# RG-LRU gates by blocks of 160 channels: permuted channels, stacked remainders, small transfers and another order of outputs

## Chip, core, metric

One Trainium2 chip, one core, one launch. The metric is the device time in microseconds (us). PE is TensorE, DVE VectorE, ACT ScalarE, POOL GpSimd, SP SyncE.

## What is computed

A two-layer network with a context of 256 tokens beside 256 latent tokens: each layer is a feed-forward half step, a mixer and another feed-forward half step, each behind a modulated norm. Layer 0's mixer is the RG-LRU, layer 1's the retention. What concerns the change is the RG-LRU, with 1280 channels in 8 gate blocks of 160:

```python
def block_diag(x, w, b):
    xg = x.reshape(bsz, t, LRU_BLOCKS, LRU_BLK)          # 8 blocks of 160
    return (jnp.einsum('btgi,gij->btgj', xg, w) + b).reshape(bsz, t, D_RNN)

def lru_coeffs(xc, gate_w, gate_b, lam):
    r = jax.nn.sigmoid(block_diag(xf, gate_w[0], gate_b[0]))
    ig = jax.nn.sigmoid(block_diag(xf, gate_w[1], gate_b[1]))
    log_a = -LRU_C * r * jax.nn.softplus(-lam)
    a = jnp.exp(log_a)
    b = jnp.sqrt(-jnp.expm1(2.0 * log_a)) * (ig * xf)
...
    # xc = conv of 4 taps over time of h @ w_x; for each of two directions d
    # h_t = a_t * h_(t-1) + b_t, the latent scan starting from the context's end
    # y = ((hs_forward + hs_backward) * gelu(h @ w_g)) @ w_out
```

## The kernel before, in words

Activations are transposed: 128 channels on the partitions, 512 columns (256 of context, 256 latent). The 1280 channels of the RG-LRU are 10 columns j of 128. Each product with a weight block is three fp32r products on PE (`mm3`, lines 142 to 144): weight high by activation high, high by low, low by high. Weights come from HBM as tiles of 8 blocks, 128x1024 (`w_fetch`, SP's queue); `w_ahead` keeps LA = 2 tiles split ahead: ACT copies the high part (`whi`, line 112), DVE subtracts for the low part (`wlo`, line 138, `w_low`). There are four buffers each of raw, high and low.

The RG-LRU stage (`lru`) runs per column: two input projections (`wx`, `wg`, 8 blocks each), a convolution of four taps (`conv`: ACT copies the sums out of PSUM into a padded buffer, line 587, and makes the first tap, line 588; DVE adds three more, line 583; ACT and DVE split the result, lines 592 and 595), the gates, ACT's functions and DVE's vector steps. Since 160 is not 128, a column of gates meets two or three columns of inputs (`gate_rows`): 26 pairs of columns, times 4 gates (r and i for two directions), times 3 products = 312. ACT's functions of a column are gelu, sigmoid (line 627), exp (632), tanh (635) and square root (642), with four loads of tables. DVE's vector steps are lines 655 to 663 with two scans (648; 650 and 651 backwards), then Y is split into high (ACT, 668) and low (DVE, 671). Of r there are three buffers, of i one, of a and s two.

The order is written by hand. Steps of ACT wait in the list `bga`, steps of DVE in `bgv`; each time PE takes up a weight block, `pump` issues one step of each list if the step's `ready` allows. So a queue's order is fixed at build time, and each engine takes its instructions in that order. The output product (`out_proj`, which adds to the residual on DVE, line 401, two halves of 256 columns) runs for columns [0, 1] before the gates of column 6, for [2 to 5] behind all gates, and for [6 to 9] as the `boundary` to the next feed-forward, by halves of 256 columns, with four weight tiles held for the second half and the statistics of the next norm (`stat`, line 311) behind it.

Of the kernel before, what the change touches and what calls it, by code (L numbers as in the profile page):

```python
# [71 lines left out]
NTILES = 371  # L72


class Kernel:
    def __init__(self, tc, aps):
        self.tc, self.nc, self.aps = tc, tc.nc, aps
# [15 lines left out]
        self.rate = 1  # L93
        self.bga, self.bgv = deque(), deque()
# [9 lines left out]
    def w_ahead(self, t):  # L104
        nc = self.nc
        self.w_fetch(min(t + LA + DA + 1, NTILES))
        while self.nsplit < min(t + LA + 1, NTILES):
# [6 lines left out]
            self.wlow.append((lo, raw, hi))  # L114
# [20 lines left out]
    def w_low(self):  # L135
        while self.wlow:
            lo, raw, hi = self.wlow.popleft()
            self.nc.vector.tensor_tensor(lo, raw, hi.bitcast(F32), ALU.subtract)  # L138
# [226 lines left out]
    def out_proj(self, acts, key, layer, gidx, halves, st=None, hooks=None, tick=0, hold=False):  # L365
# [6 lines left out]
        for hi_, (c0, c1) in enumerate(halves):  # L372
            w = c1 - c0
            def part(ps, d, lo, hi):
                for i in range(lo, hi):
                    if hi_ and hold:
                        whi, wlo = held[(i, d)]
                    else:
                        whi, wlo = held[(i, d)] = self.w(key(i, d))
                    ah, al = acts[i](c0, c1)  # L380
                    self.mm3(ps[:, :w], whi, wlo, ah, al, i == 0, i == na - 1)
            early = {}
            if hi_ == 0 and na > 1:
# [3 lines left out]
            for d in range(KD):  # L387
# [3 lines left out]
                else:  # L391
                    ps = self.psum()
                    part(ps, d, 0, na)
                if st is not None and d:
# [17 lines left out]
    def boundary(self, acts, key, layer, gidx, nl, nn, x_only=False, hold=False):  # L412
# [30 lines left out]
        self.out_proj(acts, key, layer, gidx, [(0, T), (T, 2 * T)], st=st, hold=hold, hooks={  # L443
# [98 lines left out]
    def lru(self, hooks):  # L542
        nc, tc = self.nc, self.tc
        xc, xs, gl, Y = {}, {}, {}, {}
# [15 lines left out]
        banks = self.first_group([wx(0), wx(1), wg(0), wg(1)], False, hooks)  # L560
# [6 lines left out]
        gb = self.vec("gb").rearrange("p (j g) -> p j g", j=NR)  # L567
        sp4, sp8 = self.sp4, self.sp8
        cbuf = [pool.tile([P, 2, T + 3], F32, name="cbuf%d" % i) for i in range(2)]
        for c in cbuf:  # L570
            nc.vector.memset(c[:, :, 0:1], 0.0)
            nc.vector.memset(c[:, :, T + 1:T + 3], 0.0)

        def conv(j, ps):
            buf = cbuf[j % 2]
            p3 = ps.rearrange("p (s t) -> p s t", s=2)
            x = pool.tile([P, 512], F32, tag="xc", name="xc", bufs=3)
            x3 = x.rearrange("p (s t) -> p s t", s=2)
            s = pool.tile([P, 2, 512], F32R, tag="xs", name="xs", bufs=3)
            xc[j], xs[j] = x, s  # L580

            def tap(w):
                nc.vector.scalar_tensor_tensor(x3, buf[:, :, w:w + T], cw[:, j, w:w + 1], x3,  # L583
                                               op0=ALU.mult, op1=ALU.add)

            def first():
                nc.scalar.activation(buf[:, :, 1:T + 1], p3, AF.Copy)
                nc.scalar.activation(x, ps, AF.Identity, bias=cb[:, j:j + 1], scale=cw[:, j, 1:2])
                tap(0)

            def high():
                nc.scalar.activation(s[:, 0], x, AF.Copy)

            def low():
                nc.vector.tensor_tensor(s[:, 1], x, s[:, 0].bitcast(F32), ALU.subtract)
                convdone.add(j)
            return [first, lambda: tap(2), lambda: tap(3), high, low]

        def gelu(j, ps):
            g = self.tmp("gl")  # L600
            nc.scalar.activation(g, ps, AF.Gelu_apprx_tanh)
            gl[j] = g

        def gates(j):
            rows = gate_rows(j)
            out = [self.psum() for _ in range(4)]
            for n, i in enumerate(rows):
                for dg in range(4):
                    whi, wlo = self.w(("lg", dg // 2, dg % 2, i, j))
                    if i not in convdone:  # L610
                        self.bg_until(lambda: i in convdone)
# [3 lines left out]
        def coeffs(j, ps, pgs):  # L615

            b = {}
            stt, tt = nc.vector.scalar_tensor_tensor, nc.vector.tensor_tensor
            act = nc.scalar.activation

            def new(tag, bufs):
                b[tag] = pool.tile([P, 2, 512], F32, tag=tag, name=tag, bufs=bufs)
                return b[tag]

            def sig(d, g):
                t = b[("r", "i")[g]] if d else new(*(("r", 3), ("i", 1))[g])
# [558 lines left out]
```

## Time and profile before

| | |
|---|---|
| time, median of 3 runs | 1883.34 us (1883.06 to 1883.91) |
| the profiled execution | 1883.77 us |
| its span | 1882.0 us |
| granted PE clock, mean | 0.993 |
| PE, DVE, ACT busy | 1854.5 (99%), 1283.0 (68%), 718.0 us (38%) |
| chain that ended last | PE 92%, DVE 5%, ACT 1%, issue 1% |

A busy PE is one whose products follow on one another; their ends are modelled, so their pace is read from the starts. The shares over the whole span are averages of stages with different limits: the RG-LRU stage lies from 423.6 to about 652 us of the span, and its own rows are below. A wait is the idle time of an engine ahead of an instruction, with the last instruction that released it.

### The profile page before, as it was taken

How to read it: one execution, taken by the hardware profiler on the slowest of the kernel's cores; microseconds unless marked ns; L12 is line 12 of the kernel's file. 1: busy time of each engine (PE TensorE's matmuls, PEld its weight loads, DVE VectorE, ACT ScalarE, POOL GpSimd, SP SyncE). 2: the span in 40 equal slices, each digit the busy share in tenths (PEclk: the TensorE clock that was granted, in tenths of full speed). 3: DMA queues.
4: the chain of work that ended last, by engine and by line, in shares of the span. 5: the costliest groups of instructions: out<-in, count | busy, mean ns of one | idle time of the engine just before them, and what ended most of it. 6: DMA issues, size and time to landing. Idle time of an engine off the chain costs nothing.

```text
span 1882.0 us, 25737 instructions
## 1 busy us (share of the span) xinstructions
PE 1854.5 (99%) x10282; PEld 1620.9 (86%) x10284; DVE 1283.0 (68%) x2108; ACT 718.0 (38%) x984; POOL 0.2 (0%) x4
## 2 busy tenths in 40 slices
PE   8999999999999899999999999999999999999998
PEld 7888888897888788888889888888898899999998
DVE  7877697676899975767577655455576465575555
ACT  3322222248989342222224322222243243344443
POOL 0000000000000000000000000000000000000000
PEclk8999999999999999999999999999999999999999
DMA  8355454422322244454442445454324433355553
GB/s 320 130 213 183 168 189 181 145 90 79 101 90 90 79 157 168 157 178 177 149 161 98 151 160 176 151 179 165 106 71 158 135 113 112 101 168 176 183 191 101
DMA packets 77736, 277.52 MB, mean 147 GB/s; under 512 B 8752, under 2 KB 10032, under 8 KB 77616
## 3 DMA queue, kind: packets, MB, share of 16 engines
q1 hardware_dynamic: 77616, 275.88, 42.6%
q8 instruction: 80, 1.31, 0.3%
q14 instruction: 40, 0.33, 0.1%
HBM read 274.80 MB, written 1.05 MB: 147 GB/s over the span
## 4 chain that ended last, share of the span: by engine, by line
PE 92%; DVE 5%; ACT 1%; issue 1%; DMA 0%; SPq 0%; ACTq 0%; DVEq 0%
PE ps L142 30%; PE ps L144 30%; PE ps L143 30%; PE ps L237 1%; DVE x L401 1%; DVE wlo L138 1%; DVE acc L290 1%; DVE hlo L138 1%; DVE h L360 0%; ACT h L354 0%; PE ps L335 0%; DVE ht L352 0%; PE ps L302 0%; DMA x<-xt 0%; DVE xc L583 0%
## 5 line engine op out<-in xcount | busy, mean ns | idle before, releaser
L142 PE MATMUL ps<-h,whi 128*128 128x512 f32 (+1 forms) x1824 | 640.8, 351 | 0.0
L143 PE MATMUL ps<-h,whi 128*128 128x512 f32 (+1 forms) x1824 | 640.2, 351 | 0.6 <-DVE h L360 0.5
L144 PE MATMUL ps<-h,wlo 128*128 128x512 f32 (+1 forms) x1824 | 639.5, 351 | 1.2 <-DVE wlo L138 1.2
L138 DVE TENSOR_TENSOR wlo<-wraw,whi 128x1024 fp32r<-128x1024 f32 x349 | 417.7, 1220 | 78.4 <-ACT whi L112 78.2
L112 ACT ACTIVATE whi<-wraw 128x1024 fp32r<-128x1024 f32 x349 | 357.2, 1049 | 275.4 <-PE ps L143 225.7
L144 PEld LDWEIGHTS ps<-h,wlo 128*128 128x128 f32 x1824 | 345.7, 190 | 47.7 <-DVE wlo L138 1.9
L143 PEld LDWEIGHTS ps<-h,whi 128*128 128x128 f32 x1824 | 345.7, 190 | 46.3 <-DVE h L360 1.7
L142 PEld LDWEIGHTS ps<-h,whi 128*128 128x128 f32 x1824 | 345.7, 190 | 45.2 <-ACT h L354 0.3
L242 DVE SCALAR_TENSOR_TENSOR junk<-modraw,cB 128x1024 bf16<-128x1024 f32 x240 | 293.1, 1221 | 4.6
L401 DVE SCALAR_TENSOR_TENSOR x<-ps,M,x 128x256 f32<-128x256 f32 x296 | 132.5, 479 | 159.4 <-PE ps L144 158.9
L157 ACT ACTIVATE A<-sil 128x512 fp32r<-128x512 f32 (+1 forms) x88 | 50.9, 579 | 474.3 <-DVE sil L494 474.3
L142 PE MATMUL ps<-A,whi 128*128 128x512 f32 (+1 forms) x608 | 217.9, 358 | 0.0
L143 PE MATMUL ps<-A,whi 128*128 128x512 f32 (+1 forms) x608 | 217.9, 358 | 0.0
L144 PE MATMUL ps<-A,wlo 128*128 128x512 f32 (+1 forms) x608 | 217.9, 358 | 0.0
L494 DVE TENSOR_TENSOR sil<-ps,sil 128x512 f32<-128x512 f32 (+1 forms) x88 | 54.8, 622 | 159.9 <-PE ps L144 152.0
L144 PEld LDWEIGHTS ps<-A,wlo 128*128 128x128 f32 x608 | 114.9, 189 | 17.0
L142 PEld LDWEIGHTS ps<-A,whi 128*128 128x128 f32 x608 | 114.9, 189 | 16.7
L143 PEld LDWEIGHTS ps<-A,whi 128*128 128x128 f32 x608 | 114.9, 189 | 16.7
L158 DVE TENSOR_TENSOR A<-sil,A 128x512 fp32r<-128x512 f32 (+1 forms) x88 | 55.1, 626 | 56.7 <-ACT A L157 56.7
L493 ACT ACTIVATE sil<-ps 128x512 f32<-128x512 f32 (+1 forms) x88 | 47.2, 537 | 80.4 <-PE ps L144 79.9
L354 ACT ACTIVATE h<-ht,M 128x256 fp32r<-128x256 f32 x88 | 42.4, 504 | 89.5 <-DVE ht L352 89.5
L142 PE MATMUL ps<-A,hhi 128*128 128x256 f32 x192 | 54.8, 285 | 0.0
(173 smaller groups left out, 2061.1 us busy)
## 6 DMA issues: line engine op xcount, KB each, us to landing
wraw<-w SPq DMA_DIRECT2D x371, 512.0 KB, 4.3
modraw<-modw SPq DMA_DIRECT2D x144, 512.0 KB, 4.3
x<-xt SPq DMA_DIRECT2D x8, 256.0 KB, 5.1
mask<-mask SPq DMA_DIRECT2D x4, 512.0 KB, 5.9
out<-fin SPq DMA_DIRECT2D x8, 128.0 KB, 1.8
cs<-rope SPq DMA_DIRECT2D x1, 256.0 KB, 2.6
vecs<-vecs SPq DMA_DIRECT2D x1, 251.0 KB, 6.5
ident<-ident SPq DMA_DIRECT2D x1, 64.0 KB, 2.0
```

What stands on the lines that cost most here:

```text
L112: nc.scalar.activation(hi, raw, AF.Copy)
L138: self.nc.vector.tensor_tensor(lo, raw, hi.bitcast(F32), ALU.subtract)
L142: mm(ps, whi, xhi, start=first, stop=False, skip_group_check=True)
L143: mm(ps, whi, xlo, start=False, stop=False, skip_group_check=True)
L144: mm(ps, wlo, xhi, start=False, stop=last, skip_group_check=True)
L157: self.nc.scalar.activation(hi, src, AF.Copy)
L158: self.nc.vector.tensor_tensor(lo, src, hi.bitcast(F32), ALU.subtract)
L242: nc.vector.scalar_tensor_tensor(self.junk, raw, 1.0, self.cB[:, c, :], op0=ALU.mult, op1=ALU.mult, accum_out=M[:, idx, k, c:c + 1])
L354: nc.scalar.activation(h[:, 0, a:b], tt, AF.Identity, bias=M[:, 3 * n, k, c:c + 1])
L401: nc.vector.scalar_tensor_tensor(self.x[d][:, a0:a1], ps[:, a0 - c0:a1 - c0], M[:, gidx, d, c:c + 1], self.x[d][:, a0:a1], op0=ALU.mult, o ...
L493: nc.scalar.activation(s[:, :w], pa[:, c0:c1], AF.Silu)
L494: nc.vector.tensor_tensor(s[:, :w], pg[:, c0:c1], s[:, :w], ALU.mult)
```

## The change

The channels of the RG-LRU are permuted: columns 0 to 7 are the first 128 channels of blocks 0 to 7, columns 8 and 9 the remaining 32 of blocks 0 to 3 and 4 to 7. The gates of a block are then five outputs: four of 128 (the gates) and one that holds the 32 remaining outputs of all four gates. Each gets one `mm3` from the block's own column and a single product with 96 rows from `S`, in which the 32 remainder channels stand three times (high, low, high) against weights stacked as high, high, low (kind "ls"; `w_low` makes their low part in rows 64 to 96 of the high tile, so that a weight tile with both kinds is split in two or three pieces on DVE). S is filled by three transfers of 64 KB per block and the fifth output's gates go to the remainder columns' r and i by four, all issued on POOL (56 in all). A gate is a tanh of half the argument, with the factors moved into the steps behind it; the taps of the convolution read PSUM directly; r has two buffers; three tiles are split ahead in the stage. The outputs run for [0, 1], for [2, 3, 8], for [4, 5, 6] as sums that stay in eight PSUM banks (`out_sum`), and the boundary adds [7, 9] to these, with two tiles held.

```diff
+LRU_PERM = np.concatenate([np.arange(160 * b, 160 * b + P) for b in range(8)]
+                          + [np.arange(160 * b + P, 160 * b + 160) for b in range(8)])
+LRU_ORDER = (0, 1, 2, 3, 8, 4, 5, 6, 7, 9)
...
+    def out_sum(self, acts, key):
+        banks = [self.psum() for _ in range(KD)]
+        for i, act in enumerate(acts):
+            for d in range(KD):
+                self.mm3(banks[d], *self.w(key(i, d)), *act(0, 2 * T), i == 0, False)
+        return banks
...
-        banks = self.first_group([wx(0), wx(1), wg(0), wg(1)], False, hooks)
+        banks = self.first_group([wx(8), wx(0), wx(1), wg(0)], False, hooks)
+        self.la = LA + 1
...
             def first():
-                nc.scalar.activation(buf[:, :, 1:T + 1], p3, AF.Copy)
-                nc.scalar.activation(x, ps, AF.Identity, bias=cb[:, j:j + 1], scale=cw[:, j, 1:2])
+                act(x, ps, AF.Identity, bias=cb[:, j:j + 1], scale=cw[:, j, 1:2])
                 tap(0)
...
+        def stack_x(b):
+            t = S[b] = pool.tile([P, 512], F32R, tag="S", name="S", bufs=2)
+            src = xs[8 + b // 4]
+            q = slice(32 * (b % 4), 32 * (b % 4) + 32)
+            for i, part in enumerate((0, 1, 0)):
+                nc.gpsimd.dma_start(t[32 * i:32 * i + 32], src[q, part])
...
-        def gates(j):
-            rows = gate_rows(j)
-            out = [self.psum() for _ in range(4)]
-            for n, i in enumerate(rows):
-                for dg in range(4):
-                    whi, wlo = self.w(("lg", dg // 2, dg % 2, i, j))
...
-                    self.mm3(out[dg], whi, wlo, xs[i][:, 0], xs[i][:, 1], n == 0, n == len(rows) - 1)
+        def gates(b):
+            out = [self.psum() for _ in range(5)]
+            for g in range(5):
+                self.mm3(out[g], *self.w(("lg", b, g)), xs[b][:, 0], xs[b][:, 1], True, False)
+            for g in range(5):
+                w, _ = self.w(("ls", b, g))
+                nc.tensor.matmul(out[g], w[0:96], S[b][0:96], start=False, stop=True, skip_group_check=True)
+            if b % 4 < 2:
+                stack_x(b + 2)
...
+        def gate_rem(b, ps):
+            t = self.tmp("rem")
+            act(t, ps[4], AF.Tanh, bias=self.gbr[:, b:b + 1], scale=0.5)
+            q = slice(32 * (b % 4), 32 * (b % 4) + 32)
+            for g in (0, 2, 1, 3):
+                nc.gpsimd.dma_start((R, I)[g % 2][8 + b // 4][q, g // 2], t[32 * g:32 * g + 32])
...
+            out += [with_ready(lambda: (alloc(b, R, "r", 2), gate(b, 0, ps)),
+                               lambda c: c < 2 or c - 2 in ydone, b), lambda: gate(b, 2, ps)]
...
-        out([2, 3, 4, 5])
-        js = [6, 7, 8, 9]
+        out([2, 3, 8])
...
+        js = [4, 5, 6]
+        self.bg_until(lambda: all(j in ydone for j in js))
+        banks = self.out_sum(acts(js), okey(js))
+        js = [7, 9]
...
-        self.hold |= {first + 2, first + 3, first + 6, first + 7}
-        return self.boundary(acts(js), okey(js), 0, 5, 0, 2, hold=True)
+        self.hold |= {first + 4, first + 5}
+        return self.boundary(acts(js), okey(js), 0, 5, 0, 2, hold=True, banks=banks)
```

Three places show how the rows of an engine move (line numbers of before and of the change differ). ACT's queue at the start of the stage; before, with lines 587 to 592 as the convolution:

```order
L587 ACTIVATE cbuf_3401<-ps 128x2x256
L588 ACTIVATE xc<-ps,vecs 128x512
L592 ACTIVATE xs<-xc 128x512
L587 ACTIVATE cbuf_3402<-ps 128x2x256
L588 ACTIVATE xc<-ps,vecs 128x512
L592 ACTIVATE xs<-xc 128x512
L601 ACT_TABLE_LOAD
L601 ACTIVATE gl<-ps 128x512 x2
L112 ACTIVATE whi<-wraw 128x1024 x3
```

and now, with lines 614 and 619 as the convolution, 639 as gelu:

```order
L614 ACTIVATE xc<-ps,vecs 128x512
L619 ACTIVATE xs<-xc 128x512
L614 ACTIVATE xc<-ps,vecs 128x512
L619 ACTIVATE xs<-xc 128x512
L614 ACTIVATE xc<-ps,vecs 128x512
L619 ACTIVATE xs<-xc 128x512
L639 ACT_TABLE_LOAD
L639 ACTIVATE gl<-ps 128x512
L114 ACTIVATE whi<-wraw 128x1024 x4
```

Three convolutions stand ahead of the first gelu instead of two, each without its copy, and four weight splits instead of three follow. ACT's queue at one column's functions before (627 gates, 632 exp, 635 tanh, 642 square root):

```order
L627 ACTIVATE r<-ps,vecs 128x512 x2
L627 ACTIVATE i<-ps,vecs 128x512 x2
L112 ACTIVATE whi<-wraw 128x1024
L587 ACTIVATE cbuf_3401<-ps 128x2x256
L588 ACTIVATE xc<-ps,vecs 128x512
L632 ACT_TABLE_LOAD
L632 ACTIVATE a<-r,sp_647 128x512 x2
L635 ACTIVATE r<-r,sp_646 128x512 x2
L592 ACTIVATE xs<-xc 128x512
L642 ACT_TABLE_LOAD
L642 ACTIVATE s<-r 128x1024
L112 ACTIVATE whi<-wraw 128x1024 x2
```

and now at block 3, which brings columns 3 and 8 (656 gates, 661 the fifth output, 682 exp, 685 tanh, 689 square root):

```order
L656 ACTIVATE i<-ps,gbh 128x512
L661 ACTIVATE rem<-ps,gbr 128x512
L682 ACT_TABLE_LOAD
L682 ACTIVATE a<-r,sp_647 128x512 x2
L619 ACTIVATE xs<-xc 128x512
L682 ACTIVATE a<-r,sp_647 128x512 x2
L685 ACTIVATE r<-r,sp_646 128x512 x4
L689 ACT_TABLE_LOAD
L689 ACTIVATE s<-r 128x1024
L114 ACTIVATE whi<-wraw 128x1024
L689 ACTIVATE s<-r 128x1024
L114 ACTIVATE whi<-wraw 128x1024
```

Exp, tanh and square root of two columns follow one another, and the weight splits stand behind a square root. DVE's queue there before (650 to 663 end column 2's steps, 138 is the weights' low part, 655 the first step of the next column):

```order
L650 SCALAR_TENSOR_TENSOR r<-a,s 128x256
L651 SCALAR_TENSOR_TENSOR r<-a,r,s 128x256
L662 TENSOR_TENSOR r<-r 128x512
L595 TENSOR_TENSOR xs<-xc,xs 128x512
L663 TENSOR_TENSOR r<-r,gl 128x512
L138 TENSOR_TENSOR wlo<-wraw,whi 128x1024 x2
L655 TENSOR_TENSOR i<-i,xc 128x1024
```

and now (719 to 732 end column 2's steps, 153 and 151 are the pieces of the weights' low parts, 724 is the first step of column 3):

```order
L719 SCALAR_TENSOR_TENSOR r<-a,s 128x256
L720 SCALAR_TENSOR_TENSOR r<-a,r,s 128x256
L731 TENSOR_TENSOR r<-r 128x512
L732 TENSOR_TENSOR r<-r,gl 128x512
L622 TENSOR_TENSOR xs<-xc,xs 128x512
L153 TENSOR_TENSOR wlo<-wraw,whi 128x896
L151 TENSOR_TENSOR whi<-wraw,whi 32x128
L724 SCALAR_TENSOR_TENSOR r<-a,r 128x1024
```

In place of two whole tiles, the two pieces of one split tile stand ahead of the next column's first step; the rest follows behind it.

## Rows read from the trace of the kernel before

**Rows 1.** The table of busy times by stretch, in us. Columns: stretch, its length, busy time of PE, PEld, DVE, ACT and POOL with the number of instructions in brackets, granted PE clock, DMA share, GB/s.

```profile
454.00:500.00 46.00, 46.00 (x203) 37.81 (x202) 40.36 (x45) 40.05 (x50) 0.00 (x0) 1.00 0.31 103
500.00:560.00 60.00, 60.00 (x264) 49.38 (x264) 55.75 (x72) 53.73 (x67) 0.00 (x0) 1.00 0.30 97
560.00:612.00 52.00, 52.00 (x229) 42.78 (x229) 48.70 (x59) 49.12 (x61) 0.00 (x0) 1.00 0.26 81
```

**Rows 2.** The waits from 454 to 628 us, from the first column's vector steps to the last Y: waiting engine, tile and line, what it waited for; us in total, times, longest us.

```profile
ACT Y L668 <- DVE r L663: 12.3, 1, 12.3
...
DVE wlo L138 <- ACT whi L112: 5.1, 5, 1.5
...
DVE xs L595 <- ACT xs L592: 3.4, 3, 1.6
DVE xc L583 <- ACT xc L588: 3.0, 4, 1.0
```

**Rows 3.** DVE's timeline in the first column's vector steps: start us, busy us, engine, line, operation (x2 or x3: so many in a row).

```profile
454.04 1.22 DVE L655 TENSOR_TENSOR i<-i,xc 128x1024 f32<-128x1024 f32 x1
...
462.66 1.22 DVE L138 TENSOR_TENSOR wlo<-wraw,whi 128x1024 fp32r<-128x1024 f32 x1
463.80 2.32 DVE L583 SCALAR_TENSOR_TENSOR xc<-cbuf,vecs,xc 128x512 f32<-128x512 f32 x3
466.04 0.69 DVE L663 TENSOR_TENSOR r<-r,gl 128x512 f32<-128x512 f32 x1
```

**Rows 4.** DVE's timeline around the last Y low and the first statistic of the boundary, columns as in rows 3; behind a start in square brackets the idle time before it and who ended it.

```profile
626.03 0.87 DVE L401 SCALAR_TENSOR_TENSOR x<-ps,M,x 128x256 f32<-128x256 f32 x2
626.82 0.68 DVE L671 TENSOR_TENSOR Y<-r,Y 128x512 fp32r<-128x512 f32 x1
627.42 0.87 DVE L401 SCALAR_TENSOR_TENSOR x<-ps,M,x 128x256 f32<-128x256 f32 x2
...
642.37 0.16 DVE L311 TENSOR_SCALAR rs_m<-ps 128x2 f32<-128x2 f32 x1 [0.30 <-PE ps L302]
```

**Rows 5.** PE's timeline at the start of the stage (512-column products) and at the end of the next ffn's first group (256-column products, then the next 512-column ones), columns as in rows 3. The ends of products are modelled and overlap; the starts tell the pace.

```profile
423.61 0.40 PE L142 MATMUL ps<-h,whi 128*128 128x512 f32 x1
...
424.30 0.40 PE L142 MATMUL ps<-h,whi 128*128 128x512 f32 x1
...
428.85 0.39 PE L144 MATMUL ps<-h,wlo 128*128 128x512 f32 x1
...
677.42 0.28 PE L144 MATMUL ps<-h,hlo 128*128 128x256 f32 x1
677.54 0.40 PE L142 MATMUL ps<-h,whi 128*128 128x512 f32 x1
```

**Rows 6.** ACT's timeline, columns as in rows 3: the first convolution of the stage and the start of the second, and one column's scalar steps later on (a: exp, r: tanh, s: square root).

```profile
423.87 0.60 ACT L587 ACTIVATE cbuf<-ps 128x512 f32<-128x512 f32 x1 [5.63 <-PE ps L144]
424.36 0.77 ACT L588 ACTIVATE xc<-ps,vecs 128x512 f32<-128x512 f32 x1
...
428.12 0.58 ACT L587 ACTIVATE cbuf<-ps 128x512 f32<-128x512 f32 x1
...
560.24 0.72 ACT L632 ACTIVATE a<-r,sp 128x512 f32<-128x512 f32 x1
560.85 1.33 ACT L635 ACTIVATE r<-r,sp 128x512 f32<-128x512 f32 x2
562.20 1.28 ACT L642 ACT_TABLE_LOAD   x1
563.49 1.06 ACT L642 ACTIVATE s<-r 128x1024 f32<-128x1024 f32 x1
564.46 0.61 ACT L592 ACTIVATE xs<-xc 128x512 fp32r<-128x512 f32 x1
564.98 1.99 ACT L112 ACTIVATE whi<-wraw 128x1024 fp32r<-128x1024 f32 x2
...
571.86 1.27 ACT L627 ACTIVATE r<-ps,vecs 128x512 f32<-128x512 f32 x2
573.01 1.26 ACT L627 ACTIVATE i<-ps,vecs 128x512 f32<-128x512 f32 x2
```

**Rows 7.** The groups of instructions by line and form; number of instructions, busy us, mean ns of one, idle before. The gate products of line 142 (lines 143 and 144 have as many).

```profile
L142 PE MATMUL ps<-xs,whi 128*128 128x512 f32 x104 | 41.1, 395 | 0.5 <-ACT xs L592 0.5
```

**Rows 8.** The same view, columns as in rows 7, of three kinds of DVE operation.

```profile
L401 DVE SCALAR_TENSOR_TENSOR x<-ps,M,x 128x256 f32<-128x256 f32 x296 | 132.5, 479 | 159.4 <-PE ps L144 158.9
...
L360 DVE SCALAR_TENSOR_TENSOR h<-ht,M,h 128x256 fp32r<-128x256 f32 x88 | 41.7, 481 | 8.1 <-ACT h L354 8.1
...
L658 DVE TENSOR_SCALAR a<-r 128x1024 f32<-128x1024 f32 x10 | 6.9, 687 | 0.0
```

**Rows 9.** The page's table of transfers: what, queue, number, KB each, median us from issue to landing.

```profile
out<-fin SPq DMA_DIRECT2D x8, 128.0 KB, 1.8
...
vecs<-vecs SPq DMA_DIRECT2D x1, 251.0 KB, 6.5
ident<-ident SPq DMA_DIRECT2D x1, 64.0 KB, 2.0
```

**Rows 10.** The table of busy times by stretch again, columns as in rows 1, of two stretches of 4 us at the end of the stage.

```profile
620.00:624.00 4.00, 0.67 (x3) 0.67 (x4) 3.93 (x7) 0.00 (x0) 0.00 (x0) 0.65 0.01 2
624.00:628.00 4.00, 3.86 (x18) 3.55 (x18) 3.93 (x8) 1.85 (x3) 0.00 (x0) 0.50 0.41 131
```

More of the change, by code (lines that the diff above doesn't have):

```diff
@@ L566, in lru @@
         cb = self.vec("cb")
[L567 to L572, printed above, removed]
-        def conv(j, ps):
[L575 to L580, printed above, removed]
+        gb = self.gbh.rearrange("p (j g) -> p j g", j=NR)
@@ L654, in coeffs @@
             sv = [
[L655 to L659 removed]
+                lambda: stt(r, a, 1.0, r, op0=ALU.add, op1=ALU.mult),
@@ L673, in coeffs @@
[L673 to L695 removed]
+                tt(Y[c][:, 1], r[:, 0], Y[c][:, 0].bitcast(F32), ALU.subtract)
@@ L696, in vector_steps @@
+                ydone.add(c)
+            sv[1:1], sv[5:5] = tail[:1], tail[1:]
             tail = [high, low]
             self.bgv.extend(sv)
-        for j in range(NR):
-            pgs = []
-            if j == 6:
-                out([0, 1])
-            n = j + 2 if j < 6 else j + 1
-            if j != 6 and n < NR:
-                pgs.append((n, self.proj(wg(n), 0, 2 * T)))
-            g = gates(j)
-            self.drain()
-            if prev is not None:
-                vector_steps(prev)
-            prev = coeffs(j, g, pgs)
-            self.bga.extend([lambda: None] * (3 if j else 0) + prev[0])
-            if j + 2 < NR:
-                px = self.proj(wx(j + 2), 0, 2 * T)
-                c = conv(j + 2, px)
-                rest = list(self.bgv)
-                self.bgv.clear()
-                self.bgv.extend(c[:3] + rest[:1] + c[3:4] + rest[1:2] + c[4:] + rest[2:])
@@ L718, in lru, with out @@
-        prev[1][0].ready = lambda: not self.bga
-        vector_steps(prev)
-        self.bgv.extend(tail)
-        out([2, 3, 4, 5])
-        js = [6, 7, 8, 9]
+        def out(js):
+            self.bg_until(lambda: all(j in ydone for j in js))
+            self.out_proj(acts(js), okey(js), 0, 5, [(0, 2 * T)])
+        for n, j in enumerate((8, 0, 1)):
+            self.bgv.extend(conv(j, banks[n]))
+        while self.bgv:
+            self.pump()
+        gelu(0, banks[3])
+        pgs = [(1, self.proj(wg(1), 0, 2 * T))]
@@ new lines, in lru @@
+        todo = ((("x", 2), ("g", 2)), (("x", 3), ("x", 9)), (("x", 4), ("g", 3)), (("x", 5), ("g", 8)),
+                (("x", 6), ("g", 4)), (("x", 7), ("g", 5)), (("g", 6), ("g", 7), ("g", 9)), ())
+        prev = []
+        for b in range(8):
+            if b == 6:
+                out([0, 1])
+            self.bg_until(lambda: b in convdone and 8 + b // 4 in convdone)
+            g = gates(b)
+            self.bg_until(lambda: not self.bga)
+            for c in prev:
+                vector_steps(c)
+            self.bga.extend(scalar_steps(b, g, pgs))
+            prev = [b] + ([8 + b // 4] if b % 4 == 3 else [])
+            pgs = []
+            for kind, n in todo[b]:
+                if kind == "x":
+                    c = conv(n, self.proj(wx(n), 0, 2 * T))
+                    rest = list(self.bgv)
+                    self.bgv.clear()
+                    self.bgv.extend(c[:4] + rest[:3] + c[4:] + rest[3:])
+                else:
+                    pgs.append((n, self.proj(wg(n), 0, 2 * T)))
@@ L723, in lru @@
+        out([2, 3, 8])
+        self.bg_until(lambda: not self.bga)
+        for c in prev:
+            vector_steps(c)
+        self.bgv.extend(tail)
+        self.la = LA
+        js = [4, 5, 6]
+        self.bg_until(lambda: all(j in ydone for j in js))
+        banks = self.out_sum(acts(js), okey(js))
+        js = [7, 9]
         self.drain()
```

245 lines of the change are left out of this document (139 added, 106 removed).

## Prediction

> **What bounds it now.** Three views, in this order. The table of busy times by stretch [rows 1] covers the RG-LRU stage: PE is busy in every microsecond from 454 to 612, so PE sets the pace there. The same rows put DVE at 40.36 of 46.00, 55.75 of 60.00 and 48.70 of 52.00 us: the second queue is about 90% full, and what is taken from PE can be gained only until DVE is full. The waits between the first column's vector steps and the last Y [rows 2] then say how full DVE is: in 173.4 us, from the first step at 454.04 [rows 3] to the end of the last Y low at 627.42 [rows 4], DVE waited 5.1 + 3.4 + 3.0 = 11.5 us on ACT and about 1.0 on others; 173.4 - 11.5 - 1.0 = 160.9 us is its own work. Last, the timelines [rows 3 to 6] give the length of each step. I measure from T0 = 423.61, where the stage's first 512-column product starts [rows 5]: first vector step T0 + 30.4, last Y low T0 + 203.8, first product after the next ffn's first group (677.54) T0 + 253.9.
>
> **PE.** The gates lose 312 - 160 = 152 products (104 for each of three lines before [rows 7]; now 8 blocks of 20). In a run of them the starts are 4.55 us apart for 20 intervals, from 424.30 to 428.85 [rows 5]: 0.2275 each, 152 x 0.2275 = 34.6 us; the output phases change by -0.5. If PE were still the bound the stage would end 35.1 us sooner. It can't be: DVE has some 158 us in a stretch that would be left with 138. So PE gets idle time, over 40 us of it, and while that lasts what PE does differently costs nothing. The 40 single products with 96 rows are not in this trace; I take them as 0.2275 [rows 5]. Ends: 0.12, the start spacing at the 256-column products (677.42 to 677.54 [rows 5]), and twice that 0.2275, 0.46; that is -4.3 to +9.1 us of PE time, which the idle time covers.
>
> **DVE's own work, first step to last Y low.** The nine vector steps of a column have the same sizes, the same ten times. Two more pairs of output additions fall in it (16 for 14): 0.79 a pair (626.03 to 626.82 [rows 4]), +1.6. Of the weights' low parts there are 19 whole tiles and 15 pieces of 7 more, where there were 28 tiles: 1.14 a tile (462.66 to 463.80 [rows 3]), a piece by its width plus some 0.07 to start (twice the 0.60 of 512 columns, 626.82 to 627.42 [rows 4], is 0.06 over 1.14), -1.7. One convolution fewer: three taps 2.24 (463.80 to 466.04 [rows 3]) and a low part of 0.6, -2.9. The taps now read PSUM: the addition that reads PSUM takes 479 ns, its like in SBUF 481 [rows 8], so no cost; ends 0 and, with 0.1 for each tap, +1.8. Sum: 160.9 + 1.6 - 1.7 - 2.9 = 158, rounded.
>
> **Start.** ACT and DVE take three convolutions in turn before any gate instead of two. One took 4.25 (423.87 to 428.12 [rows 6]), of which the copy into the buffer, 0.49, goes: 3.8 each, so ACT is free at T0 + 11.8 instead of T0 + 8.9. Behind it stand the table load 1.3, two gelus 1.0, five weight splits 4.75, r and i 2.3, the remainder 0.6, a load 1.3, exp 1.25, a convolution's first step 0.65, tanh 1.25, a load 1.3, square root 1.0, xs 0.6 (rows alike in [rows 6]): T0 + 29.1; two more splits 1.9, 0.35 to hand over, and three pieces on DVE, 1.3: the first vector step at T0 + 32.7, 2.3 later.
>
> **ACT's waits, the term that decides.** R has two buffers instead of three. ACT may start block b's gates only after the Y low of column b - 2, and that stands inside column b - 1's steps on DVE. ACT's queue has r, i, remainder, exp, tanh, square root and only then the weight split whose low part stands on DVE *ahead* of the next column's steps. So DVE runs out of work while ACT goes through the chain.
> - Block 3 brings two columns. ACT from the Y low: r 1.15, i 1.2, a split 0.95, first conv step 0.65, remainder 0.6, load 1.3, exp 1.24, xs 0.5, waiting for the transfers 1.0, exp of column 8 1.24, four tanh 2.5, load 1.3, square root 0.97, split 0.95: 15.6. DVE has 10.2 to do meanwhile (9.2 of work, 1.0 counted with the short waits): it waits 5.4.
> - Block 6: r 1.15, i 1.15, remainder 0.6, split 0.95, load 1.3, exp 1.24, tanh 1.24, load 1.3, root 0.97, split 0.95 = 10.85, against 7.4: 3.4.
> - Block 7, two columns again: 15.8 against 10.1: 5.7.
> - First column 2.9, and eight short waits for convolution and splits, 6.3 in all.
>
> Sum 23.7, where 11.5 was. For the transfers I take 2.0 us each, the 64 KB row in [rows 9], two behind one another; ends 1.8 and 6.5, the fastest and the slowest kind of large transfer [rows 9]. Table loads fall from 42 to 27 in the program, 15 x 1.28 = 19 us of ACT; they lie beside DVE's work except for two in each of the three chains, where I counted them.
> Last Y low: 32.7 + 158 + 23.7 + 1.0 = T0 + 215.4, **11.6 later** than T0 + 203.8.
>
> **The end of the stage.** Y low to the first statistic took 14.95 (627.42 to 642.37 [rows 4]). Now [4,5,6] are summed in eight PSUM banks beforehand and only [7,9] follow, so no third phase of additions stands behind the last Y on DVE, and two held tiles are split there instead of four: 11.4, and 32.2 instead of 34.3 for the rest, up to the next ffn's second group. Together -5.6. The engine clock is in this: PE was busy 0.67 of 4 us from 620 on and was then granted 0.50 of full speed, the lower of its two levels, from 624 to 628 [rows 10]; I assume the same for the new gap before [7,9].
>
> **Sum:** +11.6 - 5.6 = +6.0. The profiled execution took 1883.77, 0.43 over the median of 1883.34; on the median that gives 1889.3, on the profiled one 1889.8; I say **1889.5**.
>
> **The skill against the trace.** Each chain above holds two table loads at 1.28 us. In the row the load begins at 562.20, just as the tanh pair ends (560.85 + 1.33), and the root follows at 563.49 [rows 6]. The Trainium skill (ScalarE: Activation LUTs, section What ACT_TABLE_LOAD costs) has a drain of some 1.38 us beside the load's 1.28; by that each long wait would be 2.8 longer and the sum some +14. The trace shows the load but no such pause around it, so the row stands.
> Transfers issued from POOL are new; the trace of before has none. The Trainium skill (SBUF — State Buffer, box The "DVE blocks DMA" trap) says that their descriptors are written by GpSimd, which is locked out while DVE runs an operation in its fast two-port mode, and advises another queue; it speaks against this change. In this trace only the subtraction from a constant, 687 ns [rows 8] against 1.22 us for the others of that size [rows 3], looks like such a mode, once per column. That becomes a rival below.
>
> **Rivals.** All hang on w, the sum of DVE's waits on ACT: the time is 1889.5 + (w - 23.7). A measurement of this kernel tells 0.2%, 3.8 us, from no change.
> 1. *The chain as above*, w over 21.5: slower. For it: two R buffers and the split behind the root are fixed by the order. Chance 0.45; 1887 to 1897.
> 2. *Late transfers*: at 6.5 instead of 2.0 each, two in turn put 9 us more before the exponentials of column 8 and again of column 9, and DVE has nothing else: 1889.5 + 18 = 1907. It decides when a transfer of 64 KB takes over about 3. Chance 0.09.
> 3. *A smaller excess*: the slots of ACT and DVE overlap better, w from 13.9 to 21.5; within 0.2%. Chance 0.20.
> 4. *The other side: the waits stay at 11.5*, because pieces and convolutions on DVE fill the chains and ACT, with 19 us of loads and ten copies of 0.49 less, gets ahead by the time of block 3. Then Y low is at T0 + 203.2, -0.6, and with -5.6 the sum is -6.2: 1877. It decides if w is under 13.9. For it: ACT waited 12.3 in one piece for DVE already before, near the end [rows 2], so it is not always the late one; against it: the two buffers, which tie ACT to the Y low whatever else it saves. Chance 0.21.
> 5. *DVE never waits*: w = 0, -17.7, 1866; beyond it no gain is possible while DVE's 158 stand. Anything from 1873 down: 0.05.
>
> Faster 0.21 + 0.05 = 0.26, same 0.20, slower 0.45 + 0.09 = 0.54. The range 1873 to 1900 leaves out case 5 and most of case 2, and the far end of case 1. The forecast's own range is 1887 to 1897: each chain may be off by 1.5 us, the taps add up to 1.8, and a longer gap at half clock on PE some 2 more.
>
> **What would show it.** Right: PE's busy share from T0 to T0 + 215 near 77%; DVE's waits on ACT some 24 us, in three long pieces of 3 to 6 us on the weights' low part, at blocks 3, 6 and 7; ACT's r gates waiting for Y low; last Y low near 639 on the trace's clock; the next ffn's second group near 683.5; POOL's transfers near 2 us. Wrong: PE as busy as before (a product costs more than 0.2275), waits under 14 us, or POOL's transfers over 3 us with ACT's exp waiting for them. A change before 423 or behind 690 would be one that I have not seen.

## The result and the profile after

The changed kernel took 1901.82 us (median of 4, 1899.63 to 1902.13) against 1883.24: ratio 1.0096, 95% interval 1.0078 to 1.0113, **18.6 us slower**. The forecast was slower, 1889.5, 6 us over before; the measured time lies outside the range of 1873 to 1900 and the change is three times the one forecast.

The profiled execution (1902.07 us, span 1900.3) shows the loss in the RG-LRU stage. PE's first 512-column product of the stage and the one behind the next feed-forward's first group (start, length, engine, line, operation), which answer to [rows 5]:

```profile
424.12 0.40 PE L158 MATMUL ps<-h,whi 128*128 128x512 f32 x1
...
695.69 0.40 PE L158 MATMUL ps<-h,whi 128*128 128x512 f32 x1
```

271.57 us lie between them, where 253.93 did. DVE's timeline in the first column's steps, at its longest waits (idle time and releaser in square brackets), at the last Y low and the first statistic answers to [rows 3, 4]:

```profile
458.65 1.22 DVE L724 SCALAR_TENSOR_TENSOR r<-a,r 128x1024 f32<-128x1024 f32 x1
459.90 0.69 DVE L725 TENSOR_SCALAR a<-r 128x1024 f32<-128x1024 f32 x1
460.51 1.22 DVE L726 SCALAR_TENSOR_TENSOR i<-i,xc 128x1024 f32<-128x1024 f32 x1
461.76 1.23 DVE L727 TENSOR_TENSOR s<-s,i 128x1024 f32<-128x1024 f32 x1
...
521.44 1.09 DVE L153 TENSOR_TENSOR wlo<-wraw,whi 128x896 fp32r<-128x896 f32 x1 [5.68 <-ACT whi L114]
...
595.62 1.23 DVE L153 TENSOR_TENSOR wlo<-wraw,whi 128x1024 fp32r<-128x1024 f32 x1 [3.80 <-ACT whi L114]
...
608.90 0.88 DVE L428 SCALAR_TENSOR_TENSOR x<-ps,M,x 128x256 f32<-128x256 f32 x2 [5.36 <-PE ps L160]
609.70 0.68 DVE L740 TENSOR_TENSOR Y<-r,Y 128x512 fp32r<-128x512 f32 x1
...
625.73 1.23 DVE L153 TENSOR_TENSOR wlo<-wraw,whi 128x1024 fp32r<-128x1024 f32 x1 [5.23 <-ACT whi L114]
...
650.38 0.69 DVE L740 TENSOR_TENSOR Y<-r,Y 128x512 fp32r<-128x512 f32 x1 [0.69 <-ACT Y L737]
...
662.39 0.16 DVE L327 TENSOR_SCALAR rs_m<-ps 128x2 f32<-128x2 f32 x1 [0.37 <-PE ps L318]
```

From the stage's start at 424.12 the first vector step comes at +34.5 (predicted 32.7), the end of the last Y low, 650.38 + 0.61 = 650.99, at +226.9 (predicted 215.4; before 203.8). The three long waits for the weights' high part are there with almost the forecast sizes, 5.68, 3.80 and 5.23 (forecast 5.4, 3.4, 5.7). What was not forecast stands between them: 5.36 us in which DVE waits for PE at an addition of the outputs (608.90), with column 5's Y low (609.70) queued behind it. The waits between the first step and the last Y low (in all, times, longest), which answer to [rows 2]:

```profile
ACT r L656 <- DVE Y L740: 21.3, 5, 6.6
DVE wlo L153 <- ACT whi L114: 18.2, 9, 5.7
...
DVE x L428 <- PE ps L160: 5.4, 1, 5.4
...
DVE xc L611 <- ACT xc L614: 3.7, 3, 2.0
...
DVE xs L622 <- ACT xs L619: 2.3, 3, 1.4
...
DVE Y L740 <- ACT Y L737: 0.7, 1, 0.7
```

DVE's waits on ACT sum to 18.2 + 3.7 + 2.3 + 0.7 = 24.9 us (forecast 23.7, before 11.5). PE's row says why it no longer sets the pace, and in what state it is (stretch, PE, PEld, DVE, ACT, POOL busy, clock, DMA share, GB/s):

```profile
458.65:650.99 192.34, 155.66 (x614) 121.64 (x612) 159.56 (x201) 124.57 (x157) 19.66 (x40) 0.90 0.30 90
```

PE is busy 155.66 of 192.34 us at a mean granted clock of 0.90, against 1.00 in [rows 1].

### The profile page after: what moved, and what is told of

Read it like the earlier page. It is cut to its first block, busy times and chain, and to the rows that moved or that the text cites. A ratio compares the mean times of both kernels' runs of the same rounds, so it can differ in the third digit from the quotient of the medians.

```text
span 1900.3 us, 25479 instructions
## 1 busy us (share of the span) xinstructions
PE 1837.1 (97%) x10084; PEld 1598.2 (84%) x10084; DVE 1283.7 (68%) x2117; ACT 694.2 (37%) x956; POOL 27.8 (1%) x60
## 4 chain that ended last, share of the span: by engine, by line
PE 63%; DVE 6%; ACT 3%; issue 2%; DMA 0%; POOL 0%; ACTq 0%; DVEq 0%
PE ps L159 21%; PE ps L160 21%; PE ps L158 21%; DVE wlo L153 1%; ACT whi L114 1%; ACT r L685 0%; DVE i L726 0%; DVE s L727 0%; ACT h L370 0%; DVE h L376 0%; DVE r L724 0%; DVE x L428 0%; DVE hlo L153 0%; ACT a L682 0%; DVE acc L306 0%
## 5 line engine op out<-in xcount | busy, mean ns | idle before, releaser
L153 DVE TENSOR_TENSOR wlo<-wraw,whi 128x1024 fp32r<-128x1024 f32 (+2 forms) x350 | 411.7, 1199 | 88.9 <-ACT whi L114 88.4
L158 PE MATMUL ps<-Y,whi 128*128 128x512 f32 (+1 forms) x96 | 39.8, 415 | 21.0 <-DVE x L428 8.9
```

Of the source, the lines that this page charges most:

```text
L153: sub(lo[:, c], raw[:, c], hi[:, c].bitcast(F32), ALU.subtract)
L158: mm(ps, whi, xhi, start=first, stop=False, skip_group_check=True)
```

## The experiments

Each time is a median; before took 1883.2 to 1883.6 beside them. The 95% intervals of the ratios reach about 2.8 us to each side (some 1.8 with ten runs), so a difference of 1 or 2 us between two medians is not read as an effect. Theory A going in: r's two buffers tie ACT's gates to the Y low, and DVE's waits follow. Rivals: PE with its gaps and lower clock (B), ACT's own order (C).

**r freed early.**

```diff
-                               lambda c: c < 2 or c - 2 in ydone, b), lambda: gate(b, 2, ps)]
+                               lambda c: c < 2 or c - 2 in rdone, b), lambda: gate(b, 2, ps)]
...
-                lambda: tt(r[:, 0], r[:, 0], gl[c], ALU.mult),
+                lambda: (tt(gl[c], r[:, 0], gl[c], ALU.mult), rdone.add(c)),
```

> Edit: the column's last product writes into gelu's tile instead of r, Y is split from there, and r counts as free at that product, some 5 us of DVE work before the Y low. Theory A (r's two buffers tie ACT's gates to the Y low; DVE's waits, PE's gaps and the half clock follow from that): the three long waits of DVE for the weights' high part (5.7, 3.8, 5.2 us) fall under 1.5 each, DVE's waits on ACT from 24.9 to 8 to 14 us, ACT's wait for the Y low from 21 us to under 8; time 1901.8 - 12 to -20, so 1882 to 1890. Rival B (PE's half clock and its PSUM banks set the pace by themselves): PE's gaps stay, DVE waits for PE instead, time over 1896. Rival C (the weight splits behind the square root, not the buffers): the waits for the high part stay over 12 us, time over 1893.

1900.51 us: next to nothing, and theory A as put is wrong. DVE's waits on ACT are 24.5 us (24.9), 15.6 of them for the weights' high part, so by their numbers rivals B and C both still stand here. ACT's timeline around block 3's gates, first in the changed kernel, then here:

```profile
505.38 1.26 ACT L656 ACTIVATE r<-ps,gbh 128x512 f32<-128x512 f32 x2 [4.38 <-DVE Y L740]
...
513.74 1.52 ACT L682 ACTIVATE a<-r,sp 128x512 f32<-128x512 f32 x2 [0.39 <-DVE r L720]
```

```profile
503.25 1.27 ACT L656 ACTIVATE i<-ps,gbh 128x512 f32<-128x512 f32 x2 [3.50 <-DVE s L727]
...
514.45 1.53 ACT L682 ACTIVATE a<-r,sp 128x512 f32<-128x512 f32 x2 [1.83 <-DVE r L720]
```

The gates of r no longer wait for the Y low, but those of i (one buffer) wait for line 727 of the column before (3.50), which ends next to that Y low, and the exp of column 8 waits for a scan (1.83, in the changed kernel 0.39), since a has two buffers. Freeing one tie hands the wait to the next.

**Y low ahead of the additions.**

```diff
+        self.bg_until(lambda: 5 in ydone)
         out([2, 3, 8])
```

> Edit: column 5's Y low is issued before the second output phase [2, 3, 8] instead of in it, where it stood on DVE behind two additions that wait for PE. Theory A2 (the 5.4 us in which DVE waited for PE at 603.5 to 608.9 are an order of DVE's queue: the Y low, and with it block 7's gates on ACT, wait behind additions for which PE is not ready): the 5.4 us go and ACT starts block 7 some 5 us earlier; time 1901.8 - 3 to -6, 1896 to 1899. Rival B (PE at its lower clock is the limit there): the wait moves to the next additions, time within 2 us of 1901.8.

1895.68, -6.1, 0.3 below A2's range, and DVE no longer waits for PE between the first step and the last Y low. The order of DVE's queue is not shown as the only cause, since the edit also moved ACT's steps: one weight split fewer stands ahead of the gelu that PE waits for, and PE goes on to the outputs without a gap. "Two tiles split ahead", below, shows the other cause.

**Two buffers of r in the old kernel.**

```diff
-                t = b[("r", "i")[g]] if d else new(*(("r", 3), ("i", 1))[g])
+                t = b[("r", "i")[g]] if d else new(*(("r", 2), ("i", 1))[g])
```

> Edit: the kernel before with two buffers of r instead of three, nothing else. From its rows, ACT's chain from a Y low to the next column's first step is some 17.7 us where a column lasts 19.0. Theory A says that two buffers are harmless while a column lasts that long, and bind only when PE's share is gone or a block brings two columns: time within 4 us of 1883.2. Rival D (two buffers alone cost the 18 us): 1893 or more.

1896.67, +13.0: inside rival D's range, and my own expectation is wrong. The old kernel's waits between 454 and 642 us:

```profile
ACT L627 <- DVE Y L671: 27.1, 8, 9.3
DVE xc L583 <- ACT xc L588: 10.7, 6, 4.8
```

ACT waits eight times for a Y low, 27.1 us. My 17.7 us for the chain against a column of 19.0 left out that ACT's other steps then stand behind it as well: DVE's taps wait 10.7 for their first step, 3.0 before. So in the old kernel, which also has one buffer of i and two of a, the third buffer of r is worth 13.0, while in the changed kernel freeing r alone gains next to nothing.

**Twice the single products.**

```diff
+                nc.tensor.matmul(out[g], w[0:96], S[b][0:96], start=False, stop=False, skip_group_check=True)
                 nc.tensor.matmul(out[g], w[0:96], S[b][0:96], start=False, stop=True, skip_group_check=True)
```

> Edit: each of the 40 single products with 96 rows is issued twice (the gates then hold the remainder's part twice), 9.1 us of PE at full clock, up to 18 at half. Theory A (PE's idle time covers what PE does): within 2 us of 1901.8. Rival B (PE with its gaps and its lower clock is part of the chain, since ACT and DVE wait for its gates): +5 us or more.

1902.11, +0.3: 40 more products on PE are covered; PE's mean clock from the first vector step to the last Y low is 0.94 there, 0.90 without them. Rival B falls for products at the gates, not for PE's sums of the outputs.

**More buffers of r and i, and i used first.** r3i2 puts r at 3 and i at 2 buffers; glout_iq frees r as above and begins the vector steps with lines 726 and 727; both again with the Y low ahead.

```diff
-            out += [with_ready(lambda: (alloc(b, R, "r", 2), gate(b, 0, ps)),
-                               lambda c: c < 2 or c - 2 in ydone, b), lambda: gate(b, 2, ps)]
+            out += [with_ready(lambda: (alloc(b, R, "r", 3), gate(b, 0, ps)),
+                               lambda c: c < 3 or c - 3 in ydone, b), lambda: gate(b, 2, ps)]
...
-            out.append(with_ready(lambda: (alloc(b, I, "i", 1), gate(b, 1, ps)),
-                                  lambda c: c < 1 or c - 1 in ixdone, b))
+            out.append(with_ready(lambda: (alloc(b, I, "i", 2), gate(b, 1, ps)),
+                                  lambda c: c < 2 or c - 2 in ixdone, b))
```

> Edit: r has three buffers again and i two. The room comes from the conditioning copy cB, which is given up during the stage and filled with ones on POOL behind it, so the second layer's modulation is not the reference's. Theory A' (ACT is tied to DVE's column before by two things that end within 1 us of each other: r by the Y low, i by the product in line 727; freeing r alone only changes the name of the wait): DVE's waits on ACT fall from 24.9 to under 14 us, time 1901.8 - 8 to -16, 1886 to 1894. Rival C (ACT's in-order queue, with the split and the convolution's step behind exp, tanh and root, is late whatever the buffers): waits stay over 20 us, time over 1897.

> Edit: r is freed at the column's last product, as in the run before, and the vector steps begin with the two that use up i (lines 726, 727), so that i comes free some 2.4 us sooner. No more room is used and nothing is left out. Theory A': each of ACT's waits for i shrinks by 2.4, DVE's waits fall from 25 to 15 to 20 us; time 3 to 8 under the 1900.5 of r freed alone, 1892 to 1897. Rival C: within 2 us of 1900.5.

> Edit: three buffers of r and two of i (cB given up, as in r3i2), and column 5's Y low ahead of the second output phase, which alone gave -6.1. Theory A': the two add, 1880 to 1888. Rival C: 1891 to 1896, the effect of the Y low alone. Rival E (the Y low's gain was the same wait that the buffers remove): the same time as r3i2 within 2 us.

> Edit: r freed at the column's last product, i used first, column 5's Y low ahead of the second output phase; nothing left out. Theory A': 1886 to 1892. Rival C: 1893 to 1896, the effect of the Y low alone. Rival E (the same wait counted twice): the same time as glout_iq within 2 us.

1894.72, 1897.33, 1889.74 and 1892.20, each up to 1.7 above the range of theory A': two ties freed give -7.1, i used first -3.2 on glout, and the Y low's gain adds to either (-5.0, -5.1). DVE's waits on ACT fell less than theory A' said, to 20.5 in r3i2 (forecast under 14) and 21.9 in glout_iq (15 to 20). In r3i2 they fit rival C (over 20), while the time lies nearer to theory A'. Block 3's wait, 5.68, is untouched in r3i2_ylow; ACT there:

```profile
506.81 0.64 ACT L620 ACTIVATE xs<-xc 128x512 fp32r<-128x512 f32 x1 [4.37 <-DVE xc L612]
509.27 1.53 ACT L683 ACTIVATE a<-r,sp 128x512 f32<-128x512 f32 x2 [1.82 <-DVE r L721]
```

**All ties freed.** r freed at the last product, i two, a three buffers, Y low ahead; then i first as well.

```diff
-                    A[c] = pool.tile([P, 2, 512], F32, tag="a", name="a", bufs=2)
+                    A[c] = pool.tile([P, 2, 512], F32, tag="a", name="a", bufs=3)
...
-            out += [with_ready(lambda c=c: (exp(c, 0), exp(c, 1)), after(2, scandone), c) for c in cs]
+            out += [with_ready(lambda c=c: (exp(c, 0), exp(c, 1)), after(3, scandone), c) for c in cs]
```

> Edit: on the changed kernel, r freed at the column's last product, two buffers of i, three of a (cB given up as in r3i2, so the second layer's modulation is not the reference's), and column 5's Y low ahead of the second output phase. Theory A'' (block 3's wait of 5.7 us, the same in every run so far, is a third tie: exp of column 8 needs the buffer of a that column 2's scan still reads): that wait falls to 2 to 4 us, time 1885 to 1888.5. Rival C (ACT's own order: exp of column 8 stands behind xs, which waits for the taps): wait over 5 us, time within 1.5 us of r3i2_ylow's 1889.7.

> Edit: as free_all, and the vector steps begin with the two that use up i. Theory A'': with two buffers of i nothing waits for it any more, so within 1.5 us of free_all. Rival F (the order of the steps helps by itself, since a step that needs the one before it starts 1.25 us after it and another 1.14): 1.5 to 3 us under free_all.

1885.88 and 1885.46. DVE's wait at block 3 in free_all, 5.68 in every run before it:

```profile
512.11 1.09 DVE L153 TENSOR_TENSOR wlo<-wraw,whi 128x896 fp32r<-128x896 f32 x1 [0.22 <-ACT whi L114]
```

The time of free_all is in the range of theory A'', and the wait is below the 2 to 4 us that it gave. But the third buffer of a also lets the exp of column 8 be issued ahead of xs in ACT's queue, where in r3i2_ylow it stood behind xs's 4.37 and then waited 1.82 itself. Buffer and place in the queue were not tested apart. free_all_iq (-0.4) agrees with theory A''; it says nothing on rival F, since its first four steps take 4.37 us, as in the changed kernel.

**Two tiles split ahead.**

```diff
-        self.la = LA + 1
+        self.la = LA
```

> Edit: the changed kernel with weights split two tiles ahead in the stage, as before, instead of three. Theory A: the splits stand later in ACT's queue against the gates, so the waits for them grow a little: 1901 to 1906. Rival C (splits pulled ahead are what ACT's chain carries behind the root): 1895 to 1899.

1896.01, -5.8: rival C's time, and my A had the wrong sign. Rival C's reason does not show: DVE's waits on ACT are 25.6 us here, 24.9 with three tiles. The stage's start and first vector step:

```profile
425.37 0.40 PE L158 MATMUL ps<-h,whi 128*128 128x512 f32 x1
...
457.12 1.22 DVE L724 SCALAR_TENSOR_TENSOR r<-a,r 128x1024 f32<-128x1024 f32 x1
```

+31.75 instead of +34.5, and the 5.4 us for PE are gone. How, the rows of ACT, PE and DVE at the start of the outputs of [2, 3, 8] show (the rows with two times are a stretch, with columns as in [rows 1]); first the changed kernel:

```profile
599.38 1.06 ACT L114 ACTIVATE whi<-wraw 128x1024 fp32r<-128x1024 f32 x1 [2.36 <-PE ps L648]
...
602.40 0.80 PE L158 MATMUL ps<-Y,whi 128*128 128x512 f32 x1 [3.06 <-ACT gl L639]
...
608.47 0.39 PE L160 MATMUL ps<-Y,wlo 128*128 128x512 f32 x1
...
602.00:605.00 3.00, 2.60 (x6) 2.13 (x7) 1.54 (x2) 1.83 (x4) 0.00 (x0) 0.50 0.37 137
```

and with two tiles ahead:

```profile
599.13 0.50 PE L158 MATMUL ps<-Y,whi 128*128 128x512 f32 x1 [1.28 <-ACT gl L639]
...
602.44 0.39 PE L160 MATMUL ps<-Y,wlo 128*128 128x512 f32 x1
...
602.87 0.88 DVE L428 SCALAR_TENSOR_TENSOR x<-ps,M,x 128x256 f32<-128x256 f32 x2
603.66 0.68 DVE L740 TENSOR_TENSOR Y<-r,Y 128x512 fp32r<-128x512 f32 x1
...
599.00:603.00 4.00, 3.87 (x17) 3.22 (x18) 4.00 (x5) 1.57 (x4) 0.00 (x0) 1.00 0.53 190
```

With three tiles ahead a split waits 2.36 us for PE and holds up the gelu behind it. PE stands idle for that gelu for 3.06 us, and from 602 to 605 its granted clock is 0.50, the lower of its two levels: from the start of the first product to that of the 15th, at 608.47, it takes 6.07 us. With two tiles ahead PE is idle 1.28 us, the clock is 1.00, and the same starts take 3.31. The Y low stands behind the two additions in both; with the sums ready in time this order costs nothing. With the Y low ahead as well, and with all ties freed:

> Edit: the changed kernel with two tiles split ahead (alone -5.8) and column 5's Y low ahead of the second output phase (alone -6.1). In the trace of two tiles ahead the 5.4 us of DVE waiting for PE are gone too, and the stage's first vector step comes 2.8 us sooner. Theory G (the two share the 5.4; only the start is la's own): 1892 to 1894.5. Rival (they add): 1889 to 1891. Rival (they are one and the same): 1895 to 1897.

> Edit: free_all (r freed at the column's last product, i two, a three buffers, cB given up, Y low ahead) with two tiles split ahead. Theory G: only the start's 2.8 us come off free_all's 1885.9: 1882 to 1884. Rival (with the buffers free the third tile ahead pays, since ACT has room to run ahead): 1885 to 1888.

1894.84, just above theory G's range: the two overlap almost wholly, -1.2 on top of la2, since each removes the same wait. 1882.66 (ratio 0.9996, 0.9987 to 1.0006) with all ties freed, in theory G's range: the changed kernel then equals the old one. DVE's waits in it:

```profile
DVE wlo L153 <- ACT whi L114: 5.4, 3, 4.9
DVE xc L612 <- ACT xc L615: 4.4, 3, 1.7
DVE xs L623 <- ACT xs L620: 2.7, 3, 1.5
```

**The outputs.** before_sum gives the old kernel the sums in PSUM; the two others have one output phase in the changed kernel.

```diff
         out([2, 3, 4, 5])
-        js = [6, 7, 8, 9]
+        js = [6, 7]
...
+        banks = self.out_sum(acts(js), okey(js))
+        js = [8, 9]
```

```diff
-            if b == 6:
-                out([0, 1])
+            if b == 7:
+                out([0, 1, 2, 3, 8])
...
-        out([2, 3, 8])
```

> Edit: the kernel before with one part of the change alone, the outputs: [0, 1], [2 to 5], then [6, 7] as sums that stay in eight PSUM banks, and the boundary adds [8, 9] to these, with two tiles held. Theory (the end-of-stage term of the prediction, -5.6, is right and needs nothing else of the change: PE has work in the gap before the last Y and less behind it): 1877 to 1880. Rival (the gain comes only where PE has idle time long before the last Y): 1882 to 1885.

> Edit: free_all_la2 with one output phase [0, 1, 2, 3, 8] ahead of block 7's gates in place of two, [0, 1] and [2, 3, 8]: eight pairs of additions fewer on DVE, 6.3 us, and the products of [2, 3, 8], 16.4 us of PE, ahead of block 7's gates instead of behind them. Theory H (DVE is the bound once the waits are gone): 1875 to 1879. Rival B (PE brings block 7's gates late, its idle time lies elsewhere): 1882 to 1890.

> Edit: the same single output phase and two tiles ahead with r freed at the column's last product and i used first, a with two buffers, i with one; nothing left out. Theory H: 6.3 us of DVE work less than r freed, i first, Y low ahead (1892.2), and the start's 2.8: 1882 to 1886. Rival B: 1888 to 1895.

before_sum: 1886.25, +2.7, outside both ranges. PE and the first statistic there:

```profile
623.29 0.79 PE L144 MATMUL ps<-Y,wlo 128*128 128x512 f32 x1 [4.08 <-DVE wlo L138]
...
647.15 0.16 DVE L311 TENSOR_SCALAR rs_m<-ps 128x2 f32<-128x2 f32 x1 [0.36 <-PE ps L302]
```

PE still waits 4.08 us (4.26 before) for a weight's low part that stands on DVE among the last column's steps, so the sums come late and the statistic 19.8 us after the last Y low instead of 14.95. One output phase: 1894.17, 11.5 slower than free_all_la2, and 1899.52, 7.3 slower than glout_iq_ylow (which splits three tiles ahead). DVE's waits in the first of them:

```profile
DVE x L428 <- PE ps L160: 17.4, 7, 7.1
...
DVE wlo L153 <- ACT whi L114: 0.7, 3, 0.3
```

Here rival B has the direction, though both times lie over 4 us above its ranges: some 6 us of DVE work less buys 17.4 us of waiting for PE's sums. PE is busy all the time at a clock of 1.00 from 590 to 615 us there, so its idle time doesn't lie where the phase was put.

**A complete version.** All ties freed, two tiles ahead, cB through HBM and back, and independent steps next to each other.

> Edit: free_all_la2 with the conditioning copy cB written to HBM at the stage's start and read back behind it, so nothing is left out, and with the vector steps in an order in which no step needs the one just before it where that can be had (lines 724, 726, 725, 727). Theory H' (DVE's own work sets the pace once the ties are gone; a step that needs the one before it costs 0.11 to 0.25 us more): 1.5 to 3 us under free_all_la2's 1882.7, so 1879.5 to 1881.5. Rival: the reload of 1 MB behind the stage and the shift of ACT's steps take it back: 1882 to 1885.

1882.10 (ratio 0.9994, 0.9985 to 1.0004): level with the old kernel, and no run is measurably faster than that. Theory H' (1879.5 to 1881.5) missed; the time is in the rival's range. Its first steps:

```profile
455.31 1.22 DVE L727 SCALAR_TENSOR_TENSOR r<-a,r 128x1024 f32<-128x1024 f32 x1
456.44 1.22 DVE L728 SCALAR_TENSOR_TENSOR i<-i,xc 128x1024 f32<-128x1024 f32 x1
457.58 0.69 DVE L729 TENSOR_SCALAR a<-r 128x1024 f32<-128x1024 f32 x1
...
459.43 1.23 DVE L731 SCALAR_TENSOR_TENSOR s<-a,s 128x1024 f32<-128x1024 f32 x1
```

Four steps take 4.12 us (4.37 in the changed kernel, 458.65 to 463.02); over ten columns that is 2.5 us. Of these, 2.0 show in DVE's own work, the stretch from the first step to the last Y low less DVE's waits in it (161.0 us for 163.0 in free_all_la2). But the waits on ACT rise from 13.2 to 14.6, and the time falls by 0.6 only.

## Why the prediction was wrong

- **The bound was right.** PE's 34.6 us could not come through, and DVE's queue with its waits on ACT decided the sign. dup_s shows the idle time on PE, and free_all_la2 and best show that with most of the added waits gone the changed stage is worth what the old one was.
- **ACT's waits, the term that decides, had the right size and half the reason**: 24.9 against 23.7, the three chains within 0.5 us each. The text gave them to r's two buffers; glout shows that i's one and a's two take over when r is freed.
- **The step that failed: "while that lasts what PE does differently costs nothing".** DVE waited 5.36 us for PE's sums, a term that the sum had at nothing, and a Y low that ACT waits for stood behind that addition. PE's idle time was itself what made the sums late: PE stood 3.06 us for a gelu, and its products then ran at a granted clock of 0.50. out_ylow (-6.1) and la2 (-5.8) each take the wait away. I had put the additions into DVE's work at 0.79 a pair and not asked whether PE's sums were ready. This is the largest of the misses. With it falls "all hang on w": by that formula the measured w of 24.9 gives 1890.7, not 1901.8.
- **The start was 1.8 us short**: 34.5 for 32.7. ACT waited 1.4 for a raw weight tile, and exp and tanh with a second operand for the bias took 0.81 and 0.80 each, longer than in [rows 6] (0.72 for one exp, 1.33 for two tanh), as one row of ACT and the groups by line show:

```profile
445.57 1.06 ACT L114 ACTIVATE whi<-wraw 128x1024 fp32r<-128x1024 f32 x1 [1.37 <-DMA wraw<-w]
...
L682 ACT ACTIVATE a<-r,sp 128x512 f32<-128x512 f32 x20 | 15.1, 812 | 0.5 <-DVE r L720 0.4
...
L685 ACT ACTIVATE r<-r,sp 128x512 f32<-128x512 f32 x20 | 14.9, 803 | 0.0
...
L682 ACT ACT_TABLE_LOAD x7 | 9.0, 1283 | 0.1
```

  I had treated them as equal. Three tiles ahead I took as harmless; la2, with one split fewer there and no such wait, has the start 2.8 sooner.
- **DVE's own work was 3 us short**: 192.3 - 24.9 - 5.4 = 162.0, where the sum had 158 and 1.0 of other waits. The new order of the vector steps has more dependent steps in a row, 1.25 apart where independent ones are 1.14. Before, the first four took 4.12 us, from 454.04 [rows 3] to this row:

```profile
458.16 1.23 DVE L659 SCALAR_TENSOR_TENSOR s<-a,s 128x1024 f32<-128x1024 f32 x1
```

  In the changed kernel they take 4.37, 2.5 us more over ten columns; best, with another order, gets 2.0 of it back. The rest was not traced.
- **The end of the stage** was right: -5.4 us from the last Y low to the next feed-forward's second group (44.7 for 50.1), forecast -5.6, with the statistic 11.40 after (650.38 + 0.61 to 662.39). The 34.3 that the text gives for the rest of before does not come out of its rows (677.54 - 642.37 = 35.2), and the rest came as 33.3 for 32.2; the difference, which alone enters the sum, holds (-1.9 for -2.1). In the old kernel the outputs alone did not bring it, as before_sum shows.
- **Late transfers** did not come. The table of transfers:

```profile
S<-xs POOLq DMA_DIRECT2D x24, 64.0 KB, 2.0
r<-rem POOLq DMA_DIRECT2D x16, 64.0 KB, 2.3
i<-rem POOLq DMA_DIRECT2D x16, 64.0 KB, 3.0
```

  The medians are 2.0 to 3.0 us from issue to landing, issued on POOL beside DVE's work; no wait of ACT on them is among the stage's waits. The Trainium skill (SBUF — State Buffer, box The "DVE blocks DMA" trap) says that GpSimd cannot write the descriptors of its transfers while DVE runs in its two-port mode, which made this a rival at 0.09. With the one step a column that looks like that mode (0.69 us), this trace shows no such delay. The table loads stood at 1.283 us without a pause around them, as in the rows of before.

The misses sum up: 1.8 + 3.0 + 1.2 (waits on ACT) + 5.4 + 0.2 (end) + 0.5 (the stage started 0.5 later in this execution) = 12.1. Forecast were +6.0; the product behind the next feed-forward's first group came 18.1 us later than before (695.69 for 677.54).

The ledger of what undoes it, in cumulative runs: 1901.8; Y low ahead 1895.7; r 3 and i 2 buffers 1889.7; the third tie as well 1885.9; two tiles ahead 1882.7. Open: whether the Y low's place alone would have done, since out_ylow moved ACT's splits too; whether a's buffer or the exp's place ahead of xs ended block 3's wait; and why the waits on ACT rise when DVE's steps get shorter.

## What to carry to other kernels

When an engine stops being the bound, the time goes to the next queue only if the ties between the remaining engines allow it: list every buffer that one engine must give back before another can go on (here r, i and a), since the one that ends last hides those that end just before it. For each in-order queue ask what stands ahead of the instruction that others wait for, and whether that is ready. Idle time covers added work only at the place where it lies, and an engine that has idle time can still be late there.

## What the runs showed that was not expected

- Two buffers instead of three for one tile cost 13.0 us in a kernel whose PE was busy 99%.
- An exp with a scale and a bias per partition took 812 ns for 512 columns, with the scale alone 717.
- 40 products more, 9.1 us at full clock, cost 0.3 us, while a phase of 72 products put ahead of a gate cost 11.5.
- PE's mean granted clock fell from 1.00 to 0.90 in the stage, with gaps of 3 to 7 us in its work, and at the outputs of [2, 3, 8], at 0.50 from 602 to 605 us, the starts of 15 products took 6.07 us where la2 has 3.31 at 1.00. No run shows what the clock alone cost in all.
